# A hybrid decoder trunk on one core: gate and up with the normed input stationary, gated rows transposed on TensorE, the input by token tiles, the table's feedthrough diagonal on TensorE, later table pieces

## The chip, the core and the metric

The kernel runs on one core of a Trainium2 chip. A core has five engines that work side by side, each through its own queue in order: TensorE (PE; its weight loads are shown apart as PEld), VectorE (DVE), ScalarE (ACT), GpSimd (POOL) and SyncE (SP), which here only issues transfers. The kernel's matrix products go to PSUM tiles of 128 x 512 float32 numbers, called banks here. The metric is the device time of one execution in microseconds (us), as the median of several runs.

## The reference

A trunk of two layers over 256 tokens of width 1024, in float32. Each layer adds half of a SwiGLU, then a mixer, then half of a second SwiGLU, each on its RMS-normed input:

```
h = h + 0.5 * swiglu(rms_norm(h), w_gate, w_up, w_down)     # width 1024 -> 2816 -> 1024
h = h + mixer(rms_norm(h))                                  # layer 0: S5, layer 1: MoBA attention
h = h + 0.5 * swiglu(rms_norm(h), w_gate, w_up, w_down)

swiglu(h) = (silu(h @ w_gate) * (h @ w_up)) @ w_down
```

The S5 mixer is a diagonal state-space layer with 64 groups of 16 channels and 64 states each. It needs tables worked out from its parameters alone (powers of the transition, products of B and C, and a feedthrough diagonal d): they do not depend on the input. With 256 tokens the attention has one block of 256, and so is plain causal attention with 8 heads.

## The kernel before

There are six phases in a row: f00, s5, f01, f10, moba and f11, where an f phase is one SwiGLU. The 256 tokens are two tiles t of 128, the width has halves n of 512. `h` stays in SBUF.

**Precision by parts.** Every float32 operand of a large product is split into a high part, rounded to the format fp32r, and a low part, the rest. A product is then three: high x high, high x low and low x high. `Stream` (L38) brings the weights: SP loads blocks of 1 MB into three raw buffers (L163, L171, L177), `split` (L70) cuts each block in two halves and makes `whi` on ACT and `wlo` on DVE (L79 and L80; L85 and L86 where the norm's gain is multiplied in), in nine slots. `pump` (L93) places such a split ahead of need at fixed places in the program.

**An f phase.** The 2816 columns are 11 blocks j of 256. `gu` (L409) computes gate and up for half a block (f = 0, 1: 128 columns each): it goes through the eight k slices of 128 rows with the weights as the stationary operand and the transposed input `X` as the moving one, 256 tokens wide (L421 to L423). The output has columns on the partitions and tokens along the row. `act` (L431) multiplies it by the row of the norm's factors r (L433, DVE), takes silu of the gate half (L436, ACT), multiplies with the up half (L440, DVE), and makes the high and low part of the result (L448 ACT, L449 DVE), which are at once the stationary operands of the down product `dn` (L451), 512 wide, into four banks (L368 to L370). Since tokens lie along the row, r must be there as a row on all partitions: `rows_of_r` (L334) builds it once a phase with products of ones and a diagonal of r (L338). Because r enters only here, the products of a phase can begin before r is known. `act` waits for r's row only in the first block.

**Boundaries.** `boundary` (L346) finishes the four output banks of a phase in an order, adds them to h (L344) and transposes each piece of h for the next phase (L308), while PE works on the next bank.

**The tables.** They are built within f00. The generator `tables` (L499) is advanced by one step at every `fill(0.7)`, that is at every k step of `gu` and after every bank of `dn`; a counter of slots goes up by 0.7 each time. Its planner (L757 to L797) issues transfers at the slots LOADS, DVE work as a credit allows (DENSE per slot), and pieces for PE in `later`, which come LAG slots after the piece that they need and PACE slots apart. For each of eight blocks b: `muls` and `sums` (L507, DVE) give the tables' products; `spread` (L715) copies them with six ACT copies into padded tiles (L721 to L723) and stores two of them from POOL's queue (L725); `t3_tab` (L743) makes 16 small products on PE (L750), DVE adds the diagonal d, which `d_diag` makes on POOL (L739, L752), four ACT copies take the sum out (L754) and POOL stores it; `t1_tab` (L728), twice, transposes on PE (L732), copies on ACT (L734) and stores from POOL. The PE pieces write to the two `pR` banks, which `prep` shares. At the end the finished tables are loaded back by SP for the s5 phase.

**The start.** x comes in two loads of four transfers, one for each half n, both token tiles at once; `pre` transposes it on PE (L1173), and the first product follows when both halves and a few table inputs are in.

## Time and profile before

| | |
|---|---|
| time, median of 3 runs (lowest to highest) | 1079.3 us (1078.76 to 1079.53) |
| the profiled execution | 1078.01 us, span 1076.2 us |
| PE busy, share of the span | 1016.9 us, 94% |
| DVE / ACT / POOL busy | 720.6 / 570.7 / 168.2 us |
| mean granted clock of PE | 0.970 |
| read from memory | 182.84 MB, 183 GB/s over the span with what is written |

The profile is one execution. A line of a view gives a place in the kernel (L421 is its line 421), the engine, the operation, what it writes and reads, and durations. In a list of waits, "A <- B" says that A stood idle until B was done. In a timeline the first number is the start in us from the span's start, the second how long it took, and brackets hold the idle time before it. Products on PE are pipelined: a new one starts before the record of the last one ends, so their pace is read from start to start.

### The profile page before, as it was taken

The numbers are of one execution on the slowest core, as the hardware profiler recorded it, in microseconds if no ns is written. First come the engines' busy times: TensorE is split into PE (matmuls) and PEld (weight loads), VectorE is DVE, ScalarE is ACT, GpSimd is POOL, SyncE is SP. The second block draws the span as 40 slices with busy tenths as digits, with TensorE's granted clock in tenths as the row PEclk, the third lists the DMA queues.
The fourth block names the chain that finished last, engine by engine and source line by source line (L and its number), as shares of the span: only waits on it lengthen the run. The fifth ranks groups of instructions, "written<-read, shape, count | busy, mean of one in ns | idle before, by whom it ended". The sixth has DMA issues, their size and how long they took to land.

```text
span 1076.2 us, 17472 instructions
## 1 busy us (share of the span) xinstructions
PE 1016.9 (94%) x6853; PEld 935.6 (87%) x6853; DVE 720.6 (67%) x1176; ACT 570.7 (53%) x1024; POOL 168.2 (16%) x322
## 2 busy tenths in 40 slices
PE   6988888588999999999999999999999999999998
PEld 6977787577889989999998999999887889999997
DVE  5678576455687776766665776666578867766663
ACT  5444544555533355655553665554489656655451
POOL 6920110222156401000000100000044001000000
PEclk9989889799996999999999999999999999999999
DMA  8766555546765534565554566455344455665641
GB/s 242 204 189 206 177 194 179 181 161 211 280 217 209 203 134 155 201 202 187 196 169 145 171 224 231 158 197 195 122 157 157 156 157 180 221 226 163 205 142 40
DMA packets 137394, 197.64 MB, mean 184 GB/s; under 512 B 16272, under 2 KB 108896, under 8 KB 137056
## 3 DMA queue, kind: packets, MB, share of 16 engines
q1 hardware_dynamic: 133088, 183.16, 51.6%
q0 software_dynamic: 3616, 12.66, 3.5%
q8 instruction: 54, 0.88, 0.3%
q10 hardware_dynamic: 608, 0.71, 0.3%
q14 instruction: 28, 0.23, 0.1%
HBM read 182.84 MB, written 13.66 MB: 183 GB/s over the span
## 4 chain that ended last, share of the span: by engine, by line
PE 62%; POOL 2%; issue 1%; DVE 1%; ACT 0%; POOLq 0%; ACTq 0%
PE pM L422 11%; PE pM L421 11%; PE pM L423 11%; PE pA L370 7%; PE pA L368 7%; PE pA L369 7%; PE pM L368 1%; PE pM L370 1%; PE pM L369 1%; PE pR L308 1%; POOL qrs L281 1%; PE pA L934 0%; PE pA L935 0%; PE pA L933 0%; PE pR L1105 0%
## 5 line engine op out<-in xcount | busy, mean ns | idle before, releaser
L421 PE MATMUL pM<-xa,whi 128*128 128x256 f32 x1408 | 400.3, 284 | 0.0
L422 PE MATMUL pM<-xa,whi 128*128 128x256 f32 x1408 | 396.5, 282 | 0.0
L423 PE MATMUL pM<-xa,wlo 128*128 128x256 f32 x1408 | 396.0, 281 | 0.0
L86 DVE SCALAR_TENSOR_TENSOR wlo<-raw,gT,whi 128x512 fp32r<-128x512 f32 x328 | 228.1, 747 | 67.2 <-ACT whi L85 67.0
L421 PEld LDWEIGHTS pM<-xa,whi 128*128 128x128 f32 x1408 | 268.5, 191 | 4.6 <-issue 1.6
L422 PEld LDWEIGHTS pM<-xa,whi 128*128 128x128 f32 x1408 | 268.5, 191 | 3.2
L423 PEld LDWEIGHTS pM<-xa,wlo 128*128 128x128 f32 x1408 | 268.0, 190 | 0.0
L80 DVE TENSOR_TENSOR wlo<-raw,whi 128x1024 fp32r<-128x1024 f32 x156 | 195.2, 1262 | 83.0 <-ACT whi L79 81.9
L85 ACT ACTIVATE whi<-raw,gT 128x512 fp32r<-128x512 f32 x328 | 213.7, 711 | 18.2 <-PE pA L370 17.8
L79 ACT ACTIVATE whi<-raw 128x1024 fp32r<-128x1024 f32 x156 | 161.0, 1051 | 16.7 <-PE pA L934 9.8
L436 ACT ACTIVATE sg<-gr 128x256 f32<-128x256 f32 x88 | 36.8, 418 | 236.2 <-DVE gr L433 236.2
L368 PE MATMUL pA<-whi,ah 128*128 128x512 f32 x352 | 140.6, 399 | 0.0
L369 PE MATMUL pA<-wlo,ah 128*128 128x512 f32 x352 | 139.2, 396 | 0.0
L370 PE MATMUL pA<-whi,al 128*128 128x512 f32 x352 | 138.9, 395 | 0.0
L433 DVE TENSOR_TENSOR gr<-pM,rrow 128x512 f32<-128x512 f32 x88 | 60.5, 687 | 43.6 <-PE pM L423 43.3
L448 ACT ACTIVATE ah<-act 128x256 fp32r<-128x256 f32 x88 | 36.8, 418 | 82.1 <-DVE act L440 82.1
L370 PEld LDWEIGHTS pA<-whi,al 128*128 128x128 f32 x352 | 67.1, 191 | 14.7
L368 PEld LDWEIGHTS pA<-whi,ah 128*128 128x128 f32 x352 | 67.3, 191 | 11.1 <-issue 0.2
L369 PEld LDWEIGHTS pA<-wlo,ah 128*128 128x128 f32 x352 | 67.3, 191 | 10.8
L323 POOL TENSOR_TENSOR ms<-ss 128x1 f32<-128x1 f32 x10 | 1.9, 193 | 476.5 <-ACT sq L320 476.5
L449 DVE TENSOR_TENSOR al<-act,ah 128x256 fp32r<-128x256 f32 x88 | 37.4, 425 | 42.6 <-ACT ah L448 42.6
L440 DVE TENSOR_TENSOR act<-gr,sg 128x256 f32<-128x256 f32 x88 | 37.3, 424 | 26.5 <-ACT sg L436 26.5
(239 smaller groups left out, 1208.9 us busy)
## 6 DMA issues: line engine op xcount, KB each, us to landing
raw<-in_ffn_w_down_dram SPq DMA_DIRECT2D x44, 1024.0 KB, 5.1
raw<-in_ffn_w_gate_dram SPq DMA_DIRECT2D x80, 512.0 KB, 3.8
raw<-in_ffn_w_up_dram SPq DMA_DIRECT2D x80, 512.0 KB, 4.8
raw<-in_moba_w_qkv_dram SPq DMA_DIRECT2D x12, 1024.0 KB, 5.1
TB<-dB SPq DMA_DIRECT2D x8, 768.0 KB, 6.9
raw<-in_ffn_w_gate_dram SPq DMA_DIRECT2D x16, 256.0 KB, 4.2
raw<-in_ffn_w_up_dram SPq DMA_DIRECT2D x16, 256.0 KB, 4.5
dB<-tt POOLq DMA_DIRECT2D x16, 256.0 KB, 3.0
```

What stands on the lines that cost most here:

```text
L79: nc.scalar.activation(hi, r, AF.Copy)
L80: nc.vector.tensor_tensor(lo, r, hi.bitcast(F32), op=OP.subtract)
L85: nc.scalar.activation(hi[:, c], r[:, c], AF.Identity, scale=g)
L86: nc.vector.scalar_tensor_tensor(lo[:, c], r[:, c], g, hi[:, c].bitcast(F32), op0=OP.mult, op1=OP.subtract)
L368: mm(o, xh, wh, start=start, stop=False)
L369: mm(o, xh, wl, start=False, stop=False)
L370: mm(o, xl, wh, start=False, stop=stop)
L421: mm(o, a, xh, start=k == 0 and i == 0, stop=False, skip_group_check=True)
L422: mm(o, a, xl, start=False, stop=False, skip_group_check=True)
L423: mm(o, b, xh, start=False, stop=k == 7, skip_group_check=True)
L433: V.tensor_tensor(gr, ps.rearrange("p (i c) -> p i c", i=2), Rr["row"][:, None, :].to_broadcast([128, 2, 256]), op=OP.mult)
L449: V.tensor_tensor(al, a, ah.bitcast(F32), op=OP.subtract)
```

## The change

In an f phase, gate and up of a whole block are computed for one token tile at a time: a slice of `X` (128 rows, 128 tokens) is the stationary operand, and 512 weight columns (256 of gate, 256 of up) move past it. `gu(j, t)` takes the place of `gu(j, f)`. Tokens now lie on the partitions, so r is a number for each partition: it is the scale of silu and a factor in the DVE product that makes `act`; the diagonal and the row of r are gone. The gated rows must be turned before the down product: `tr(j, t)` transposes two 128 x 128 pieces on PE into a `pR` bank, from which ACT and DVE make the high and low parts. It stands at k = 6 of the next pass of `gu`. Of the down products, `dn(j - 2, 1)` now follows the first pass of block j and `dn(j - 1, 0)` the second.

All boundaries go by token tile, with a call for the last transpose between. x is loaded by token tiles, the first one over SP and ACT, and the products of the first tile start before the second tile is prepared, which is done in hooks of the first pass.

In the tables, the diagonal is made at the head of `spread` in two buffers and added by four small products on PE; `spread(b - 1)` comes behind the first `muls` of block b; the second half of the powers E comes last rather than after block 2; LAG is 12 rather than 9, PACE 4 rather than 3, the loads come at slots 2 to 24 rather than 3 to 36, and the generator is advanced only after slot 3. The offsets of the operands within their SBUF tiles change (XO, AO, OO).

```diff
--- before.py
+++ after.py
-XO = {'f00': 8, 's5': 124, 'g': 0, 'f01': 88, 'f10': 8, 'moba': 124, 'f11': 8}
-AO = (76, 76, 76, 76)
-OO = 76
-
-SC = (0, 0, 2, 3, 4)
-
-LOADS, C_AT, E_AT, B_AT, DENSE, LAG, PACE = (3, 6, 9, 12, 15, 18, 21, 24, 27, 30, 33, 36), 40, 26, 36, 0.46, 9, 3.0
+XO = {'f00': 124, 's5': 124, 'g': 0, 'f01': 116, 'f10': 124, 'moba': 124, 'f11': 124}
+AO = (116, 116, 116, 116)
+OO = 116
+
+LOADS, C_AT, E_AT, B_AT, DENSE, LAG, PACE = (2, 4, 6, 8, 10, 12, 14, 16, 18, 20, 22, 24), 42, 26, 36, 0.46, 12, 4.0
...
+    h2 = cp.tile([128, 2, D], F32, name="h2")
+    h = [h2[:, t, :] for t in range(2)]
+
+    def rows(t, s, c0, nc_):
+
+        return [(t * 128 + s) * D + c0, [[4 * D, 32], [1, nc_]]]
+
+    def ld_x(t, engines):
+        for s in range(4):
+            off, ap = rows(t, s, 0, D)
+            engines[s % len(engines)].dma_start(h2[s * 32:s * 32 + 32, t, :],
+                                                bass.AP(tensor=x.tensor, offset=x.offset + off, ap=ap))
+
+    ld_x(0, [nc.sync, nc.scalar])
     nc.scalar.dma_start(gn[0:32], ffn_norm.rearrange("l i (k p) -> (l i k) p", p=128))
     nc.scalar.dma_start(gn[32:48], mix_norm.rearrange("l (k p) -> (l k) p", p=128))
     warm(AF.Exp)
-    h2 = cp.tile([128, 2, D], F32, name="h2")
...
-    def diag_of_r():
-        for t in range(2):
-            Rr["diag", t] = sp.tile([128, 128], F32, name="rdiag", tag="rdiag", bufs=2)
-            nc.vector.tensor_scalar(Rr["diag", t], ident, Rr[t], None, op0=OP.mult)
-
-    def rows_of_r():
-
-        ps = psR()
-        for t in range(2):
-            mm(ps[:, t * 128:(t + 1) * 128], ones, Rr["diag", t], start=True, stop=True)
-        Rr["row"] = sp.tile([128, 256], F32, name="rrow", tag="rrow", bufs=1)
-        nc.vector.tensor_copy(Rr["row"], ps[:, 0:256])
...
-    def boundary(nxt, parts, acc, scale):
-
-        if nxt is not None and nxt[0] == "f":
-            order = [(0, 0), (1, 0), (0, 1), (1, 1)]
-        else:
-            order = [(0, 0), (0, 1), (1, 0), (1, 1)]
-        for part in parts[:-1]:
-            part(*order[0])
-            part(*order[1])
+    def boundary(nxt, parts, acc, scale, mid=None):
+
+        order = [(0, 0), (0, 1), (1, 0), (1, 1)]
+        for i in range(2):
+            for part in parts[:-1]:
+                part(*order[i])
+            if mid is not None and i == 0:
+                mid()
         for i, (t, n) in enumerate(order):
             for part in parts[-1:] if i < 2 else parts:
                 part(t, n)
...
-    def ffn(tag, nxt, entry, fill, fill0=()):
+    def ffn(tag, nxt, entry, fill):
+
         V = nc.vector
         acc = [None] * 4
-        AT = {}
-
-        def gu(j, f, hooks):
+        AT, AC = {}, {}
+
+        def gu(j, t, hooks):
             us = [where[tag, "g", j, a] for a in range(2)]
             ps = psM()
+            ts = slice(t * 128, t * 128 + 128)
             for k in range(8):
                 for fn in hooks.get(k, ()):
                     fn()
+                fill(0.7)
                 wh, wl = st.get(us[k // 4], (k % 4) // 2)
-                xh, xl = X["h"][:, k, :], X["l"][:, k, :]
-                for i in range(2):
-                    c = (k % 2) * 512 + i * 256 + f * 128
-                    o = ps[:, i * 256:(i + 1) * 256]
-                    a, b = wh[:, c:c + 128], wl[:, c:c + 128]
-                    mm(o, a, xh, start=k == 0 and i == 0, stop=False, skip_group_check=True)
-                    mm(o, a, xl, start=False, stop=False, skip_group_check=True)
-                    mm(o, b, xh, start=False, stop=k == 7, skip_group_check=True)
+                c = slice((k % 2) * 512, (k % 2) * 512 + 512)
+                mm3(ps, X["h"][:, k, ts], X["l"][:, k, ts], wh[:, c], wl[:, c], k == 0, k == 7)
                 if k % 2:
-                    if k < 7 and (j, f, k) not in ((0, 0, 1), (L, 1, 5)):
+                    if k < 7 and (j, t, k) not in ((0, 0, 1), (L, 1, 5)):
                         st.pump()
-                    if f == 1:
+                    if t == 1:
                         st.release(us[k // 4], (k % 4) // 2)
-            return ps
-
-        def act(j, f, ps):
-            gr = fp.tile([128, 2, 256], F32, name="gr", bufs=2)
-            V.tensor_tensor(gr, ps.rearrange("p (i c) -> p i c", i=2),
-                            Rr["row"][:, None, :].to_broadcast([128, 2, 256]), op=OP.mult)
             sg = fp.tile([128, 256], F32, name="sg", bufs=1)
-            nc.scalar.activation(sg, gr[:, 0, :], AF.Silu)
-            if (j, f) != (L, 1):
+            nc.scalar.activation(sg, ps[:, 0:256], AF.Silu, scale=Rr[t])
+            if (j, t) != (L, 1):
                 st.pump()
-            a = fp.tile([128, 256], F32, name="act", bufs=1)
-            V.tensor_tensor(a, gr[:, 1, :], sg, op=OP.mult)
-            if f == 0:
+            AC[t] = fp.tile([128, 256], F32, name="act", bufs=2)
+            V.scalar_tensor_tensor(AC[t], ps[:, 256:512], Rr[t], sg, op0=OP.mult, op1=OP.mult)
+
+        def tr(j, t):
+            if t == 0:
                 AT[j] = []
                 for i, n in enumerate(("ah", "al")):
                     o = AO[2 * i + j % 2]
                     a2 = fp.tile([128, 640], F32R, name=n, bufs=2)
                     AT[j].append(a2[:, o:o + 512].rearrange("p (f c) -> p f c", c=256))
-            ah, al = (x[:, f, :] for x in AT[j])
-            nc.scalar.activation(ah, a, AF.Copy)
-            V.tensor_tensor(al, a, ah.bitcast(F32), op=OP.subtract)
+            ps = psR()
+            pv = ps[:, 0:256].rearrange("p (f c) -> p f c", c=128)
+            a = AC.pop(t)
+            for f in range(2):
+                nc.tensor.transpose(pv[:, f, :], a[:, f * 128:(f + 1) * 128], ident)
+            ah, al = (x[:, :, t * 128:t * 128 + 128] for x in AT[j])
+            nc.scalar.activation(ah, pv, AF.Copy)
+            V.tensor_tensor(al, pv, ah.bitcast(F32), op=OP.subtract)
 
         def dn(j, f):
             u = where[tag, "d", j]
@@ -461,36 +442,21 @@
                 st.pump()
 
         L = NJ - 1
-        fills = {k: [lambda: fill(0.7)] for k in range(8)}
         for j in range(NJ):
+            h0 = dict(entry) if j == 0 else {6: [lambda: tr(j - 1, 1)]}
             if j == 0:
-                if fill0:
-                    p0 = gu(0, 0, fills)
-                    h1 = {k: list(v) for k, v in fills.items()}
-                    h1[1].append(diag_of_r)
-                    h1[2].append(lambda: warm(AF.Silu))
-                    h1[3].append(rows_of_r)
-                    h1[4].append(lambda: act(0, 0, p0))
-                    act(0, 1, gu(0, 1, h1))
-                    continue
-                hooks = {}
-                for k, fn in zip(SC, (lambda: None, lambda: None, diag_of_r, lambda: warm(AF.Silu), rows_of_r)):
-                    hooks.setdefault(k, []).append(fn)
-                p0 = gu(0, 0, entry)
-                hooks[rows_at := SC[4]].append(lambda: act(0, 0, p0))
-                p1 = gu(0, 1, hooks)
-                act(0, 1, p1)
-                continue
-            act(j, 0, gu(j, 0, fills))
-            dn(j - 1, 0)
-            act(j, 1, gu(j, 1, fills))
-            if j < L:
-                dn(j - 1, 1)
+                h0.setdefault(5, []).append(lambda: warm(AF.Silu))
+            gu(j, 0, h0)
+            if j > 1:
+                dn(j - 2, 1)
+            gu(j, 1, {6: [lambda: tr(j, 0)]})
+            if j:
+                dn(j - 1, 0)
 
         def part(j, f):
             return lambda t, n: bank_mm(acc, t, n, *AT[j], where[tag, "d", j], [f], False, (j, f) == (L, 1))
 
-        boundary(nxt, [part(L - 1, 1), part(L, 0), part(L, 1)], acc, 0.5)
+        boundary(nxt, [part(L - 1, 1), part(L, 0), part(L, 1)], acc, 0.5, lambda: tr(L, 1))
...
         def spread(b):
 
+            d_diag(b)
...
+        DG = {}
+
         def d_diag(b):
-            dg = tp.tile([32, 4, 32], F32, name="dg", tag="dg", bufs=1)
-            P.tensor_tensor(dg, ident[0:32, None, 0:32].to_broadcast([32, 4, 32]),
+            DG[b] = tp.tile([32, 4, 32], F32, name="dg", bufs=2)
+            P.tensor_tensor(DG[b], ident[0:32, None, 0:32].to_broadcast([32, 4, 32]),
                             dTq[0:32, 4 * b:4 * b + 4, None].to_broadcast([32, 4, 32]), op=OP.mult)
-            return dg
 
         def t3_tab(b):
             t3 = t3s[b % 2]
-            dg = d_diag(b)
             ps = psR()
             pk = ps[0:32].rearrange("p (q t c) -> p q t c", q=4, c=32)
             for qq in range(4):
                 for i in range(2):
                     mm(ps[0:32, qq * 128:(qq + 1) * 128], MPs[b % 2][:, i, qq, 3].rearrange("p g n -> p (g n)"),
-                       TTs[b % 2][:, i, qq, 0:4].rearrange("p t g n -> p (t g n)"), start=i == 0, stop=i == 1)
-            V.tensor_tensor(pk[:, :, 0, :], pk[:, :, 0, :], dg, op=OP.add)
+                       TTs[b % 2][:, i, qq, 0:4].rearrange("p t g n -> p (t g n)"), start=i == 0, stop=False,
+                       skip_group_check=True)
+                mm(pk[:, qq, 0, :], ident[0:32, 0:32], DG[b][:, qq, :], start=False, stop=True,
+                   skip_group_check=True)
             for s in range(4):
                 nc.scalar.activation(t3[32 * s:32 * s + 32, :, s:4, :], pk[:, :, 0:4 - s, :], AF.Copy)
             nc.gpsimd.dma_start(dB[b][:, 1024:1536], t3.rearrange("p q t c -> p (q t c)"))
...
-        def add_e(hf):
+        def add_e(hf, b=None):
             at = E_AT
-            for c, f in ((0.6, (e_init, hf)), (0.5, (e_step, 1)), (0.6, (e_step, 2)), (0.8, (e_step, 4)),
...
-                         (1.3, (e_step, 32, 8, 8, 0)), (0.9, (e_step, 32, 8, 8, 1)), (0.0, (e_store, hf))):
+                         (1.3, (e_step, 32, 8, 8, 0)), (0.9, (e_step, 32, 8, 8, 1)), (0.0, (e_store, hf)))):
+                if b is not None and i == 3:
+                    add_spread(b)
                 work.append((c, at, f, (), -4))
+
+        def add_spread(b):
+            work.append((0.0, B_AT, (spread, b), [(t3_tab, b), (t1_tab, b, 0), (t1_tab, b, 1)], 3 * (b - 1)))
 
         add_e(0)
         for k, w in enumerate((1.2, 1.2, 1.4)):
             work.append((w, B_AT, (b_all, k), (), -4))
         for b in range(NB):
-            for w, f in ((1.2, (muls, b, 0)), (1.2, (muls, b, 1)), (0.7, (sums, 0)), (0.7, (sums, 1))):
-                work.append((w, B_AT, f, (), 0))
-            work.append((0.0, B_AT, (spread, b), [(t3_tab, b), (t1_tab, b, 0), (t1_tab, b, 1)], 3 * (b - 1)))
-            if b == 2:
-                add_e(1)
+            for w, f in ((1.2, (muls, b, 0)), (None, b - 1), (1.2, (muls, b, 1)), (0.7, (sums, 0)), (0.7, (sums, 1))):
+                if w is not None:
+                    work.append((w, B_AT, f, (), 0))
+                elif b:
+                    add_spread(b - 1)
+        add_e(1, NB - 1)
...
     def fill(dt):
         slot[0] += dt
-        next(tab, None)
+        if slot[0] > 3.0:
+            next(tab, None)
...
+    for n in range(2):
+        squares(0, n)
+        pre(0, n)
     st.pump()
     busy(4)
     next(tab, None)
+    first = {1: [lambda: pre(1, 0)], 3: [lambda: pre(1, 1)], 5: [lambda: squares(1, 0)], 6: [lambda: squares(1, 1)]}
 
     for i, ph in enumerate(phases):
         nxt = phases[i + 1] if i + 1 < len(phases) else None
         if ph[0] == "f":
-            ffn(ph, nxt, entry_hooks(ph), fill,
-                not i)
+            ffn(ph, nxt, entry_hooks(ph) if i else first, fill)
```

37 lines of the change are left out of this document (2 added, 35 removed).

## The prediction

> **What bounds the kernel now.** The page comes first: the busy shares, the granted clock in 40 slices, and the costliest group.
>
> ```profile
> span 1076.2 us, 17472 instructions
> PE 1016.9 (94%) x6853; PEld 935.6 (87%) x6853; DVE 720.6 (67%) x1176; ACT 570.7 (53%) x1024; POOL 168.2 (16%) x322
> PEclk9989889799996999999999999999999999999999
> L421 PE MATMUL pM<-xa,whi 128*128 128x256 f32 x1408 | 400.3, 284 | 0.0
> ```
>
> TensorE (PE) is the bound, and its clock dips only in the first third. The windows by stage say where (columns: stretch, busy time of PE, PEld, DVE, ACT and POOL, granted clock, DMA share, GB/s).
>
> ```profile
> 19.00:60.00 41.00, 41.00 (x304) 39.55 (x304) 27.90 (x48) 20.47 (x28) 37.46 (x88) 0.96 0.77 219
> 60.00:262.00 202.00, 163.48 (x1087) 148.50 (x1086) 127.26 (x191) 103.46 (x180) 32.42 (x49) 0.90 0.56 185
> 400.00:586.00 186.00, 186.00 (x1339) 174.96 (x1338) 122.48 (x182) 99.12 (x164) 4.87 (x14) 1.00 0.54 182
> 586.00:773.00 187.00, 186.91 (x1344) 175.30 (x1342) 126.80 (x188) 100.17 (x167) 4.87 (x14) 1.00 0.56 187
> ```
>
> The feed-forward phases f01 and f10 run with PE full at clock 1.00, 186 us each. The first one, f00, does the same products and lasts to about 280: it also builds the S5 tables, and from 60 to 262 PE is idle 38.5 us of 202. The waits of PE between 19 and 262 (longest in total first; total, times, longest):
>
> ```profile
> PE pR L732 <- ACT t L754: 23.2, 5, 7.7
> PE pR L750 <- ACT mp L723: 6.5, 2, 4.6
> PE pR L696 <- DMA cn<-in_s_c_re_dram: 4.5, 1, 4.5
> PE pR L732 <- ACT t L734: 4.3, 2, 2.2
> ```
>
> These four sum to 38.5 us. The longest one in the timeline, engine by engine, and the clock just around it:
>
> ```profile
> 189.24 0.61 ACT L723 ACTIVATE mp<-zc 64x512 f32<-64x512 f32 x1
> 189.63 1.49 POOL L725 DMA_DIRECT2D dB<-tt  x2 [10.57 <-ACT tt L722]
> 191.13 0.41 POOL L739 TENSOR_TENSOR dg<-cst,dTq 32x128 f32<-32x128 f32 x1
> 191.58 0.29 DVE L752 TENSOR_TENSOR pR<-pR,dg 32x128 f32<-32x128 f32 x1 [4.26 <-POOL dg L739]
> 191.90 1.74 ACT L754 ACTIVATE t<-pR 32x512 f32<-32x512 f32 x4 [2.05 <-DVE pR L752]
> 193.69 1.12 PE L732 MATMUL pR<-cst,mp 128*128 128x128 f32 x4 [7.69 <-ACT t L754]
> 189.90:196.70 6.80, 3.01 (x12) 2.86 (x13) 2.24 (x3) 4.74 (x8) 2.78 (x5) 0.50 0.37 120
> ```
>
> The reader is to see a chain over four engines: the diagonal dg stands on POOL behind the stores of the next piece (L725), those wait for ACT's copies, DVE adds dg, ACT copies the sum out, and only then has PE a free pR bank. After the wait the clock stands at 0.50. Over 60 to 262 the clock costs 202 x (1 - 0.90) = 20.2 us more. So the tables cost f00 about 38.5 + 20.2 = 58.7 us.
>
> **The change part by part.** *Gate and up with 512 columns.* Start to start, the 256-wide products take (643.54 - 639.80) / 32 = 0.1169 us, the 512-wide ones (1071.59 - 1069.08) / 11 = 0.2282 us:
>
> ```profile
> 639.80 0.28 PE L421 MATMUL pM<-xa,whi 128*128 128x256 f32 x1
> 643.54 0.28 PE L423 MATMUL pM<-xa,wlo 128*128 128x256 f32 x1
> 1069.08 0.39 PE L368 MATMUL pA<-whi,ah 128*128 128x512 f32 x1
> 1071.59 0.40 PE L370 MATMUL pA<-whi,al 128*128 128x512 f32 x1
> ```
>
> 3 x 1408 = 4224 narrow products become 2112 wide ones: 2112 x (0.2338 - 0.2282) = -11.8 us, all on PE's path.
>
> *Transposes of the gated rows.* New: 11 blocks x 2 token tiles x 4 phases = 88 pairs. What a pair, a reciprocal-row product (L338, four passes) and a group of 16 table products (L750) cost in PE's stream:
>
> ```profile
> 367.73 0.39 PE L916 MATMUL pR<-cst,gs 128*128 128x128 f32 x2
> 367.87 0.36 PE L933 MATMUL pA<-xa,whi 128*128 128x256 f32 x1
> 368.07 0.28 PE L934 MATMUL pA<-xa,whi 128*128 128x256 f32 x1
> 414.97 0.61 PE L338 MATMUL pR<-rdiag,ones 128*128 128x128 f32 x4
> 415.33 0.37 PE L421 MATMUL pM<-xa,whi 128*128 128x256 f32 x1
> 415.54 0.28 PE L422 MATMUL pM<-xa,whi 128*128 128x256 f32 x1
> 177.82 1.94 PE L750 MATMUL pR<-tt,mp 128*32 128x128 f32 x16 [1.96 <-ACT mp L723]
> 179.69 0.50 PE L368 MATMUL pA<-whi,ah 128*128 128x512 f32 x1
> ```
>
> The pair holds PE 0.14 us and makes the next product 0.20 instead of 0.117: 0.223 us, so 88 x 0.223 = +19.6. The Trainium skill's page "TensorE: Matmul & The Clock Gate", Part 4 (PE-mode transpose), speaks against the change: it gives about 275 ns for a 128x128 transpose in a kernel's context. By that the 176 transposes would be 48.4 us, and the sum 28.8 us worse; the rows above do not agree, since two of them pass in 0.22 us.
>
> *Removed with the rows of r.* Four groups of L338, each 0.36 + (0.21 - 0.117) = 0.45: -1.8 us. The DVE multiply by the row (L433) goes too, but PE was full in f01 and f10, so that time is worth nothing there; what it frees is order, below.
>
> *Diagonal on PE.* 32 small products at (179.69 - 177.82) / 16 = 0.117: +3.7 us. In exchange DVE's add leaves the chain, and dg is made at the start of spread, ahead of the stores L725 on POOL. The 23.2 us wait loses its mechanism.
>
> *Later pieces.* A spread (six ACT copies, then stores) moves behind the next block's first multiply, so ACT meets sums that DVE finished earlier; pieces follow 12 slots after it rather than 9, 4 apart rather than 3 (0.7 slot is one k step, 0.68 us). This takes the ground from the 6.5 and 4.3 us waits. The twelve small loads on SP come up to twelve slots earlier, the C loads at 18 to 24 for a use at 42 instead of 27 to 36 for 40: the 4.5 us wait should go. They queue ahead of weight blocks on SP, hidden behind three raw buffers. I take the whole -38.5 and the clock's -20.2, with half as the poor end.
>
> *The wait that is new.* The pair stands at k = 6 of the next pass, 6 x 3 x 0.2282 = 4.1 us after the pass ended, and waits for act (DVE), itself behind sg and the weight split pumped between them. In f01 that chain looks so:
>
> ```profile
> 515.93 0.69 DVE L433 TENSOR_TENSOR gr<-pM,rrow 128x512 f32<-128x512 f32 x1 [0.60 <-PE pM L423]
> 516.71 0.42 ACT L436 ACTIVATE sg<-gr 128x256 f32<-128x256 f32 x1 [2.64 <-DVE gr L433]
> 517.78 1.41 DVE L86 SCALAR_TENSOR_TENSOR wlo<-raw,gT,whi 128x512 fp32r<-128x512 f32 x2 [1.16 <-ACT whi L85]
> 519.11 0.41 DVE L440 TENSOR_TENSOR act<-gr,sg 128x256 f32<-128x256 f32 x1
> 186.17 0.29 ACT L721 ACTIVATE tt<-cb 64x128 f32<-64x128 f32 x1
> 187.35 0.63 ACT L722 ACTIVATE tt<-zc 64x512 f32<-64x512 f32 x1 [0.89 <-DVE zc L507]
> 41.87 3.63 DVE L80 TENSOR_TENSOR wlo<-raw,whi 128x1024 fp32r<-128x1024 f32 x3 [0.52 <-ACT whi L79]
> ```
>
> From sg's start to act's end 519.52 - 516.71 = 2.8 us, so 1.3 us of slack for the first token tile; the second has the twelve products of a dn (2.7 us) more before its pair. In f00 a spread holds ACT from 186.17 to 189.85, 2.8 us without the 0.89 that it waits for DVE. If all of that stood ahead of sg, PE would wait 1.5 us; behind the pair stand the last two k steps, and behind its copies ah and al ACT's next splits. I let half of the eight spreads hit, 4 x 1.5 = +6 us; the ends are 0 and, with the three splits of the row at 41.87 ahead of act in some twenty early and table passes, 20 x (3.6 - 1.3) = +46.
>
> *Start and SBUF offsets.* The products begin when both halves of x and the table inputs are in:
>
> ```profile
> 11.54 1.94 PE L1173 MATMUL pA<-cst,h 128*128 128x128 f32 x8 [2.86 <-DMA h<-in_x_dram]
> 18.80 0.39 PE L421 MATMUL pM<-xa,whi 128*128 128x256 f32 x1
> ```
>
> With token tile 0 first, they could begin near 12 (up to -6.8), but then stop for the second tile and each split (1.05 on ACT, 1.22 on DVE for a third of a pass), at half clock; and two of the four loads now stand on ACT's queue ahead of gn. I take 0, ends -6.8 and +3.5. The offsets (XO, AO, OO), the order at the boundaries, where the second token tile is now wanted one pass later, and the loads of finished tables, which SP issues nearer to the end of f00: nothing in the rows prices them; 0, ends +-3, an estimate of 1 us for each.
>
> Sum against the profiled execution's 1078.0: -38.5 - 20.2 - 11.8 + 19.6 - 1.8 + 3.7 + 6 = -43.0, so **1035 us**. The median of the runs is 1.3 us above that execution, within the rounding of this sum.
>
> **The rivals.**
> - *Half of the table waits stay*, because ACT's queue, not POOL's, is what is late: half of 58.7 comes back, 1035 + 29 = 1064, less the 6 counted already: 1058. For it: ACT does splits, sg, spreads and pieces in one queue. Against: it is busy only 103 of 202 us, and the waits end at DVE and POOL rows.
> - *A pair of transposes drains PE* rather than streams: 0.39 us each, the whole record of the pair at 367.73, 88 x (0.39 - 0.22) = +15: 1050. Against: the next product starts at 367.87. The Trainium skill's figure for a transpose, named above, points the same way and would make 1064.
> - *The change does not do what it says*: every table wait stays, as the two pR banks now also serve the 22 pairs of f00. Only the PE terms remain: -11.8 + 19.6 - 1.8 + 3.7 = +9.7, so 1088.
> - *Slower: act is late for the pair in all four phases.* At each of the 44 first-tile passes three splits stand before act: 44 x (3.6 - 1.3) = 101 us over my sum without the 6, 1130. It decides from 49 / 44 = 1.1 us a pass. For it: in f00 DVE did stand behind three splits at 41.87, and the order sg, split, act is kept. Against: ACT no longer waits for DVE's gr, and in f01 the chain takes 2.8 us.
>
> **How the numbers follow.** The forecast 0.70 (its own range 1022 to 1050), half of the waits 0.12, draining pairs 0.05, no table gain 0.05, late act 0.08. The range 1020 to 1062 holds the first three, 0.87, less tails of the start and the residual waits. A change of less than 0.2% is about what cannot be told from none. Faster 0.86, same 0.01, slower 0.13.
>
> **What would show it.** Right: the f00 stage ends near 232 instead of 280; granted clock near 1.00 after 60; no wait of PE on L754's successor; 512-wide gate and up products about 0.228 apart; each pair near 0.22; f01, f10 and f11 about 1.5 us longer each. Wrong: PE waits on act at the transposes beyond a few us, or table waits with another releaser and the clock still at 0.90.

## The result and the profile after

The changed kernel takes 1066.1 us, the kernel before 1079.3 us: a ratio of 0.988 (95% interval 0.986 to 0.990). It is faster by 13 us where I had forecast 44, and 1066.1 lies outside my range of 1020 to 1062 us.

From the page of the changed kernel, the line of TensorE's busy time and the granted clock in 40 slices:

```profile
PE 1024.5 (96%) x4965; PEld 844.7 (79%) x4965; DVE 655.0 (62%) x1068; ACT 579.2 (54%) x1024; POOL 152.1 (14%) x329
...
PEclk9779999999988999999999999999999999999999
```

TensorE is still the bound. The dips of the clock have moved to the second and third slices, 27 to 80 us; the later dip, in s5, is in both kernels. The windows of the changed kernel say the same (columns as in the prediction):

```profile
13.00:62.00 49.00, 25.78 (x85) 17.85 (x85) 17.68 (x25) 16.81 (x27) 28.71 (x99) 0.74 0.46 128
62.00:250.00 188.00, 188.00 (x954) 149.08 (x953) 131.73 (x197) 116.36 (x196) 30.34 (x48) 0.99 0.69 228
```

From 62 us on, the table building that had cost the kernel before its idle time and its clock costs nothing more: PE is busy for all of 188 us (62 to 250), at clock 0.99. But from 13 to 62 us PE works only 25.8 of 49 us. There stand these waits of PE in the changed kernel (13 to 290 us; total, times, longest):

```profile
PE pR L427 <- DVE act L414: 16.0, 1, 16.0
PE pM L351 <- ACT whi L77: 5.0, 4, 1.8
PE pM L352 <- DVE wlo L78: 2.2, 4, 0.8
```

One wait holds two thirds of it. Where the stages end is read from the last four preparation transposes at each boundary (end of f00, s5, f01; timeline of PE, kernel before):

```profile
287.11 0.60 PE L308 MATMUL pR<-cst,h 128*128 128x128 f32 x4
407.37 0.60 PE L308 MATMUL pR<-cst,h 128*128 128x128 f32 x4
593.79 0.60 PE L308 MATMUL pR<-cst,h 128*128 128x128 f32 x4
```

and in the changed kernel:

```profile
271.80 0.49 PE L305 MATMUL pR<-cst,h 128*128 128x128 f32 x3
391.14 0.60 PE L305 MATMUL pR<-cst,h 128*128 128x128 f32 x4
579.08 0.60 PE L305 MATMUL pR<-cst,h 128*128 128x128 f32 x4
```

The start with f00 is shorter by 15.3 us (287.1 to 271.8), s5 by 0.9, f01 is longer by 1.5 (186.4 to 187.9). The later stages, read in the same way, are +1.4 (f10), +0.1 (moba) and +1.6 (f11). So the three f phases behind f00 came out as forecast, and the stretch up to the end of f00 is the place of the error: -47.5 forecast (-58.7 for waits and clock, +1.5 for the PE terms of a phase, +3.7 diagonal, +6 for the new wait), -15.3 measured.

### The profile page after: what moved, and what is told of

Its sections match the earlier page's. It is cut to its first block, busy times and chain, and to the rows that moved or that the text cites. A ratio compares the mean times of both kernels' runs of the same rounds, so it can differ in the third digit from the quotient of the medians.

```text
span 1064.7 us, 13634 instructions
## 1 busy us (share of the span) xinstructions
PE 1024.5 (96%) x4965; PEld 844.7 (79%) x4965; DVE 655.0 (62%) x1068; ACT 579.2 (54%) x1024; POOL 152.1 (14%) x329
## 4 chain that ended last, share of the span: by engine, by line
PE 87%; POOL 5%; DVE 3%; issue 3%; ACT 1%; DMA 1%; ACTq 0%; SPq 0%; POOLq 0%; DVEq 0%
PE pM L351 16%; PE pM L352 16%; PE pM L353 16%; PE pA L351 9%; PE pA L353 9%; PE pA L352 9%; PE pR L427 2%; PE pR L717 2%; PE pM L820 1%; PE pR L305 1%; POOL qrs L278 1%; PE pA L908 1%; PE pA L909 1%; PE pA L910 1%; DMA h<-in_x_dram 1%
## 5 line engine op out<-in xcount | busy, mean ns | idle before, releaser
L351 PE MATMUL pM<-whi,xa 128*128 128x512 f32 x832 | 342.1, 411 | 5.0 <-ACT whi L77 5.0
L352 PE MATMUL pM<-wlo,xa 128*128 128x512 f32 x832 | 328.7, 395 | 2.2 <-DVE wlo L78 2.2
L353 PE MATMUL pM<-whi,xa 128*128 128x512 f32 x832 | 327.8, 394 | 0.0
L83 ACT ACTIVATE whi<-raw,gT 128x512 fp32r<-128x512 f32 x328 | 217.2, 714 | 71.6 <-PE pA L353 62.5
L351 PEld LDWEIGHTS pM<-whi,xa 128*128 128x128 f32 x832 | 158.2, 190 | 35.4 <-ACT whi L77 6.7
L353 PEld LDWEIGHTS pM<-whi,xa 128*128 128x128 f32 x832 | 157.9, 190 | 34.7
L352 PEld LDWEIGHTS pM<-wlo,xa 128*128 128x128 f32 x832 | 158.4, 190 | 32.4 <-DVE wlo L78 4.1
L429 ACT ACTIVATE ah<-pR 128x256 fp32r<-128x256 f32 x88 | 33.7, 383 | 128.9 <-PE pR L427 128.7
L410 ACT ACTIVATE sg<-pM,rr 128x256 f32<-128x256 f32 x88 | 41.7, 474 | 97.1 <-PE pM L353 76.9
L430 DVE TENSOR_TENSOR al<-pR,ah 128x256 fp32r<-128x256 f32 x88 | 37.0, 421 | 72.7 <-ACT ah L429 72.7
L414 DVE SCALAR_TENSOR_TENSOR act<-pM,rr,sg 128x256 f32<-128x256 f32 x88 | 42.3, 480 | 46.9 <-ACT sg L410 46.9
L427 PE MATMUL pR<-cst,act 128*128 128x128 f32 x176 | 33.9, 274 | 16.0 <-DVE act L414 16.0
```

The costliest lines, as they stand in the source:

```text
L83: nc.scalar.activation(hi[:, c], r[:, c], AF.Identity, scale=g)
L351: mm(o, xh, wh, start=start, stop=False)
L352: mm(o, xh, wl, start=False, stop=False)
L353: mm(o, xl, wh, start=False, stop=stop)
L410: nc.scalar.activation(sg, ps[:, 0:256], AF.Silu, scale=Rr[t])
L414: V.scalar_tensor_tensor(AC[t], ps[:, 256:512], Rr[t], sg, op0=OP.mult, op1=OP.mult)
```

## The experiments

None of the fifteen kernels leaves out a part of the reference. The time of the kernel before beside them was 1078.0 to 1079.2 us.

### r of token tile 1 ahead of the tables

The 16 us wait, followed back in the timeline of the changed kernel:

```profile
27.80 0.45 POOL L513 TENSOR_TENSOR e<-prm 128x32 f32<-128x32 f32 x2 [12.53 <-DVE dTq L504]
...
56.29 0.20 POOL L320 TENSOR_TENSOR ms<-ss 128x1 f32<-128x1 f32 x1
...
58.33 0.19 POOL L282 TENSOR_TENSOR rr<-rr,rs_e 128x1 f32<-128x1 f32 x1
58.56 0.47 ACT L410 ACTIVATE sg<-pM,rr 128x256 f32<-128x256 f32 x1 [17.94 <-POOL rr L282]
...
61.68 0.69 PE L427 MATMUL pR<-cst,act 128*128 128x128 f32 x2 [16.01 <-DVE act L414]
```

ACT's sg of the second token tile waits 17.9 us for r of that tile, POOL computes it at 56.3 to 58.5, and until then POOL works through the parameters of the tables, begun at 27.8 us. In the changed kernel the squares of tile 1 are issued at k = 5 and 6 of the first pass, and the parameters' chain, all of it at once, at k = 5, just ahead of the last square. The edit lets the chain come later:

```diff
-        if slot[0] > 3.0:
+        if slot[0] > 4.5:
             next(tab, None)
```

> Edit: the changed kernel with the gate of fill at slot 4.5 instead of 3.0, so that POOL computes r of token tile 1 (L320, L321, rsq) ahead of the table parameters' chain and not behind it; nothing else moves but the three first steps of the tables, by two k steps. POOL theory: the 16.0 us wait of PE for act before the second pair of transposes is the wait for r of tile 1, and the 2.7 us of half clock behind it are its echo; both go, 18.7 us, so 1066.1 - 18.7 = 1047 us, and the chain of waits at 62 us has no L414. Rival, late splits: in the first passes DVE and ACT are behind with splits and table work anyway, act comes little earlier, and the time stays above 1060. Rival, displaced chain: the parameters are ready later and the first E pieces or the dB stores wait in turn, 1052 to 1058.

Measured: 1047.4 us (ratio 0.971, 0.970 to 0.973), 18.7 us less than the changed kernel. The timeline of this run:

```profile
30.08 0.62 POOL L320 TENSOR_TENSOR ms<-ss 128x1 f32<-128x1 f32 x1 [14.44 <-ACT sq L317]
...
32.67 0.44 POOL L513 TENSOR_TENSOR e<-prm 128x32 f32<-128x32 f32 x2
```

POOL makes r at 30 us and begins the parameters behind it. What is left of waits for act (L414) is 1.9 us in two places. The chain of tables begins 5 us later, and no table wait comes up for it (the waits of PE from 13 to 290 us are those for act and for the first pass's splits). The POOL theory holds in full; both rivals are out.

### The two halves of the change, each alone at the old start

The change has a feed-forward part and a table part; both with the kernel before's start (x by halves, both tiles prepared and r computed ahead of the first pass). First the whole change at the old start:

```diff
-    ld_x(0, [nc.sync, nc.scalar])
+    ld_x(0, [nc.sync])                  # x by halves of 512 columns, as before
...
-    for n in range(2):
-        squares(0, n)
-        pre(0, n)
+    for t in range(2):
+        square(t, 0)
+    pv = [pre(t, 0) for t in range(2)]
...
```

> Edit: the changed kernel with the start of the kernel before: x by halves of 512 columns for both token tiles, both tiles prepared ahead of the first pass, r of both in one POOL chain ahead of the table parameters. Gate and up, transposes and tables stay changed. By the trace, TensorE lost 20.3 us up to 45 us in the changed kernel and 10.4 in the kernel before, so the start by token tiles costs 9.9 us beside the wait for r. Theory: 1066.1 - 18.7 - 9.9 = 1037.5 us. Rival, the start by token tiles is not at fault (the lateness is that of the weights): 1047 us, as with r alone.

Then the tables alone, in the kernel before:

```diff
-LOADS, ... = (3, 6, ..., 36), 40, 26, 36, 0.46, 9, 3.0
+LOADS, ... = (2, 4, ..., 24), 42, 26, 36, 0.46, 12, 4.0
...
+            d_diag(b)
             tv, mv = ...
...
-            V.tensor_tensor(pk[:, :, 0, :], pk[:, :, 0, :], dg, op=OP.add)
+                mm(pk[:, qq, 0, :], ident[0:32, 0:32], DG[b][:, qq, :], start=False, stop=True, ...)
...
+                    add_spread(b - 1)
```

> Edit: the kernel before with the table part of the change alone: the diagonal on TensorE, dg ahead of the stores, spreads one multiply later, the new LOADS, C_AT, LAG and PACE, the gate of fill; to fit in SBUF dtb and dg share two buffers. Gate and up stay as they were (256 columns, r's rows by TensorE). Theory of the double count: between 60 and 290 us the kernel before lost 50.4 us against the usual cadence, 38.5 of it waits and about 12 the half clock while TensorE was busy (my 20.2 also counted the half clock under the waits); so 1079.3 - 50 + 3.7 for the diagonal = 1033 us. Rival, the sum as predicted: 1079.3 - 58.7 + 3.7 = 1024 us. Rival, the tables gain only because the changed feed-forward relieves ACT and DVE: 1050 us or more.

And the feed-forward part alone (the same lines of tables undone in the run with the old start):

> Edit: the kernel before with the feed-forward part alone: gate and up with the normed input stationary, gated rows transposed on TensorE, the boundary order and the SBUF offsets of the changed kernel; start and tables as before. By the terms of the sum: -11.8 for the wide products, +19.6 for the pairs, -1.8 for the rows of r, so 1079.3 + 6 = 1085 us if the table waits stay what they were. Rival: without the multiply by r's row on DVE and with act on one engine less, table waits shrink by themselves: 1060 to 1075 us. Rival: the pair's copies make ACT and DVE later for the tables: 1090 us or more.

| at the old start | tables before | tables changed |
|---|---|---|
| feed-forward before | 1078.5 | 1042.0 (0.966, 0.965 to 0.967) |
| feed-forward changed | 1061.4 (0.984, 0.982 to 0.985) | 1045.1 (0.969, 0.967 to 0.970) |

All three sums missed. The whole change at the old start was expected at 1037.5 us and takes 1045.1. The tables alone bring 36.5 us, not 46 or 55. The feed-forward alone, which I had priced as a loss of 6 us, brings 17. Together they bring less than the tables alone, but that comparison is not clean: both kernels of the lower row lose some 5 us in f01 and f10 for a reason of their own (f01 lasts 191.5 us in each of them, 187.9 in the changed kernel), which the next section takes up. Without that loss the whole change at the old start takes 1039.1 us, 3 us less than the tables alone. The waits of PE in the run with the feed-forward alone (60 to 262 us):

```profile
PE pR L699 <- ACT t L721: 11.6, 4, 4.2
PE pR L699 <- DVE al L431: 4.7, 2, 2.5
```

Of 38.5 us of table waits 16.3 are left with the old tables: the rival "without the multiply by r's row the waits shrink by themselves" holds. The two halves of the change take away the same waits, so their gains, 36.5 and 17 us, do not add up, with 1039.1 us either. Which part of the feed-forward shrinks the waits was not run apart. And in the run with the tables alone a wait has come up that neither kernel has, PE for ACT's copies of C's transposes (60 to 290 us):

```profile
PE pR L696 <- ACT cb L699: 10.5, 2, 7.5
```

In that run TensorE loses 12 us against its usual cadence between 60 and 80 us, so by that estimate the tables alone would stand near 1030 us without it; the run that tried to get there, further down, did not.

The longer f01 is the next experiment.

### Where the operands lie in SBUF

In the run with the old start nothing of f01 had been edited, but 512-wide products came 0.233 us apart: (452.00 - 449.90) / 9 in its timeline,

```profile
449.90 0.39 PE L354 MATMUL pM<-whi,xa 128*128 128x512 f32 x1
...
452.00 0.40 PE L354 MATMUL pM<-whi,xa 128*128 128x512 f32 x1
```

against (452.83 - 450.09) / 12 = 0.228 us in the changed kernel:

```profile
450.09 0.39 PE L351 MATMUL pM<-whi,xa 128*128 128x512 f32 x1
...
452.83 0.39 PE L351 MATMUL pM<-whi,xa 128*128 128x512 f32 x1
```

What differs is that the start before holds its squares and r in small tiles of its own, ss4, ms2 and rr2, in the pool that lies ahead of the feed-forward's. Two runs test it. One makes the old start with the changed kernel's small tiles:

```diff
-    ss4 = sp.tile([128, 2, 2], F32, ...); def square(t, n): ...
-    for t in range(2):
-        square(t, 0)
+    for t in range(2):
+        squares(t, 0)
...
-    v2, r2 = ...; rsq(r2, v2, 2)
```

> Edit: as the run with the old start, but the squares and r of both tiles are made by the changed kernel's own function, so that the pool of small tiles, which lies in SBUF ahead of the pool of ah and al, keeps its size. In the run with the old start the stages f01, f10 and f11 were 5.1, 2.8 and 3.0 us longer than before instead of 1.5, 1.4 and 1.6, and the down products came every 232 to 238 ns instead of 227 to 229, though nothing there had been edited. Placement theory: about 40 bytes more in the small pool moved ah and al against the place that the offsets AO were set for; with the old size the three stages come back to +1.5 and the run to 1045.1 - 6.7 - some 2 in f00 = 1036 us, and the start by halves is worth 1047.4 - 1036 = 10 us or a little more. Rival: the cadence is set by something else (which weight buffers the stages meet after another start), the stages stay at +5.1 and +2.8, 1045 us.

The other takes the run of 1047.4 us and gives it the old offsets:

```diff
-XO = {'f00': 124, 's5': 124, 'g': 0, 'f01': 116, 'f10': 124, 'moba': 124, 'f11': 124}
-AO = (116, 116, 116, 116)
-OO = 116
+XO = {'f00': 8, 's5': 124, 'g': 0, 'f01': 88, 'f10': 8, 'moba': 124, 'f11': 8}
+AO = (76, 76, 76, 76)
+OO = 76
```

> Edit: the changed kernel with r of tile 1 ahead of the tables (the run of 1047.4 us), and in it the offsets XO, AO and OO of the kernel before, nothing else. My prediction took them at 0 with ends of 3 us. Placement theory: offsets and pools belong together, so the old offsets in the new pools give the 232 to 238 ns cadence in some of the stages; from 1 to 5 us for each of f00, f01, f10 and f11, 1051 to 1067 us. Rival, offsets without weight: 1047 us, and all cadences 227 to 229.

Measured: 1039.1 us (0.963, 0.961 to 0.965) for the first, 6 us less than with the old small tiles and 3 more than expected; 1059.6 us (0.982, 0.980 to 0.983) for the second, 12.2 us more than with the new offsets, where nothing but the offsets was edited. The ends of s5 and f01 with the old start and the changed kernel's small tiles,

```profile
363.01 0.49 PE L306 MATMUL pR<-cst,h 128*128 128x128 f32 x3
...
550.90 0.49 PE L306 MATMUL pR<-cst,h 128*128 128x128 f32 x3
```

with the old start and its own small tiles,

```profile
362.85 0.49 PE L306 MATMUL pR<-cst,h 128*128 128x128 f32 x3
...
554.35 0.60 PE L306 MATMUL pR<-cst,h 128*128 128x128 f32 x4
```

and with the old offsets:

```profile
373.99 0.49 PE L305 MATMUL pR<-cst,h 128*128 128x128 f32 x3
...
564.79 0.49 PE L305 MATMUL pR<-cst,h 128*128 128x128 f32 x3
```

f01 takes 187.9, 191.5 and 190.8 us. So the small tiles, by my count of their sizes a shift of some tens of bytes, cost 3.6 us in a stage of 188, and the line of offsets in the diff, priced by me at 0 with ends of 3 us, keeps 12 us. It isn't a gain over the kernel before, whose cadence was 0.228 too: the offsets go with the pools, and whoever changes the pools has to set them anew. What in the address decides was not tried.

The same two runs price the start: 1047.4 - 1039.1 = 8.3 us between the start by token tiles and the start by halves, r's wait left out. (The first slots of the tables differ by two k steps between them as well.)

### What the start by token tiles costs

The first pass in the run of 1047.4 us: first product, one of the stops for splits, first pair of transposes.

```profile
15.70 0.50 PE L351 MATMUL pM<-whi,xa 128*128 128x512 f32 x1 [1.77 <-ACT whi L77]
26.37 0.50 PE L351 MATMUL pM<-whi,xa 128*128 128x512 f32 x1 [1.33 <-ACT whi L77]
36.96 0.33 PE L427 MATMUL pR<-cst,act 128*128 128x128 f32 x1 [0.39 <-DVE act L414]
```

and in the placed run with the start by halves:

```profile
14.49 0.77 PE L352 MATMUL pM<-whi,xa 128*128 128x512 f32 x1
...
26.80 0.38 PE L428 MATMUL pR<-cst,act 128*128 128x128 f32 x2
```

The first products differ by 1.2 us, the first pairs by 10.2. Two runs, each with one edit to the run of 1047.4 us, ask whether the loads or the order of preparation do it:

```diff
-    ld_x(0, [nc.sync, nc.scalar])
     nc.scalar.dma_start(gn[0:32], ...)
     nc.scalar.dma_start(gn[32:48], ...)
+    ld_x(0, [nc.sync, nc.scalar])
```

> Edit: the changed kernel with r of tile 1 ahead of the tables (1047.4 us), and in it the two gn loads stand ahead of the two x loads on ACT's queue, as in the kernel before. In the run of 1047.4 us the first transpose of gn comes at 10.0 us and the first product at 15.7; in the placed run with the old start they come at 5.9 and 14.5, and the first pair of transposes at 36.96 and 26.80. Theory, order of preparation: the loads carry no more than the 1.2 us between the first products, since TensorE then stops for ACT's and DVE's splits; 1046 to 1048 us. Rival, loads: gn four us earlier brings everything forward, 1042 to 1044 us.

```diff
+    for n in range(2):
+        squares(1, n)
+        pre(1, n)
     st.pump()
     busy(4)
     next(tab, None)
-    first = {1: [lambda: pre(1, 0)], 3: [lambda: pre(1, 1)], 5: ..., 6: ...}
+    first = {}
```

> Edit: the changed kernel with r of tile 1 ahead of the tables (1047.4 us), and in it the squares and the preparation of token tile 1 stand ahead of the first pass, behind those of tile 0; x still comes by token tiles on two queues. Theory, order of preparation: in the first pass ACT and DVE have only the splits left, so TensorE goes through without stops and at full clock, as in the start by halves; 4 to 8 us of the 8 come back: 1039 to 1043 us. Rival, loads: tile 1 comes last on SP, the first product moves to 18 us or more, and what the pass gains the later beginning takes: 1046 to 1049 us.

Measured: 1046.5 us with gn first (0.970, 0.969 to 0.971), 1043.4 with both tiles ahead (0.967, 0.966 to 0.969). With gn first, the first product and the first pair:

```profile
13.52 0.79 PE L351 MATMUL pM<-whi,xa 128*128 128x512 f32 x1 [1.77 <-ACT whi L77]
...
36.60 0.38 PE L427 MATMUL pR<-cst,act 128*128 128x128 f32 x2
```

The products begin 2.2 us earlier and the pass ends 0.4 earlier: the stops for the splits take it back. With both tiles ahead:

```profile
19.38 0.67 PE L351 MATMUL pM<-whi,xa 128*128 128x512 f32 x1 [5.21 <-ACT whi L77]
...
33.88 0.44 PE L427 MATMUL pR<-cst,act 128*128 128x128 f32 x2 [0.39 <-DVE act L414]
```

the products begin 3.7 us later and the pass ends 3.1 earlier. So of the 8.3 us, 4 come back when tile 1 is prepared ahead of the first pass, in which it had held up ACT's and DVE's splits; the queue place of gn is worth 1 us at most. The other 4 are a difference, not an experiment of their own: I put them to x by token tiles, whose second tile comes last, and that is not shown.

### What took the table waits away

My argument was the diagonal: dg made ahead of the stores on POOL, no add on DVE. The edit makes the diagonal as in the kernel before, in the run of 1047.4 us:

```diff
-            d_diag(b)                                    # in spread
...
+            dg = d_diag(b)                               # in t3_tab
-                mm(pk[:, qq, 0, :], ident[0:32, 0:32], DG[b][:, qq, :], start=False, stop=True, ...)
+            V.tensor_tensor(pk[:, :, 0, :], pk[:, :, 0, :], dg, op=OP.add)
```

> Edit: the changed kernel with r of tile 1 ahead of the tables (1047.4 us), and in it the diagonal of D as in the kernel before: dg made by POOL in t3_tab, added by DVE, no products for it on TensorE. The later pieces, LAG and PACE stay. Theory of my prediction: dg behind the stores on POOL and DVE's add make the copy late for the pR bank, so a part of the 23.2 us comes back, against 3.7 us of products saved: 1050 to 1066 us, with waits of PE for L720's successor. Rival: it was the spacing (12 slots after the spread, 4 apart) that took the waits away, and the diagonal on TensorE only costs: 1047.4 - 3.7 = 1043.7 us.

Measured: 1040.3 us (0.964, 0.962 to 0.965), 7.1 us faster than with the diagonal on TensorE. The rival holds, and by more than it asked. The pieces of one block in TensorE's timeline, from their first product to the first one behind them, with the diagonal on TensorE:

```profile
109.04 0.62 PE L717 MATMUL pR<-tt,mp 128*32 128x128 f32 x4
109.60 0.24 PE L720 MATMUL pR<-dg,cst 32*32 32x32 f32 x2
...
111.95 0.50 PE L351 MATMUL pM<-whi,xa 128*128 128x512 f32 x1
```

and with it on DVE, and the group of the successor in that run (60 to 290 us; busy, mean ns of one, idle before it):

```profile
110.82 1.93 PE L716 MATMUL pR<-tt,mp 128*32 128x128 f32 x16
112.69 0.50 PE L351 MATMUL pM<-whi,xa 128*128 128x512 f32 x1
...
L698 PE MATMUL pR<-cst,mp 128*128 128x128 f32 x64 | 9.7, 274 | 0.3 <-ACT t L720 0.3
```

The waits do not come back: 0.3 us before the successor. And the diagonal lengthens a block's piece from 1.87 to 2.91 us, so eight blocks by 8.3 us. Each product of these small ones leaves two records (the 16 records of a block are eight products in the program), so the 32 products of the diagonal are 64 records, at 0.13 us each. The best parts together, the placed run with the start by halves and this diagonal:

> Edit: the run with the old start and the placed pools (1039.1 us), and in it the diagonal on DVE as in the kernel before. The diagonal on TensorE cost 1047.4 - 1040.3 = 7.1 us in the other start. Theory, the parts add up: 1039.1 - 7.1 = 1032 us, without waits of PE in the table pieces. Rival: with the products 8 us earlier the DVE add stands behind splits and the pieces wait, 1036 us or more.

Measured: 1030.6 us (0.956, 0.955 to 0.958), against 1032 expected. The parts add up, and this version beats both kernels. From there two runs undo the planner's changes, one each:

```diff
-... 0.46, 12, 4.0
+... 0.46, 9, 3.0
```

> Edit: the best parts (wide gate and up, old start, placed pools, diagonal on DVE), and in it LAG 9 and PACE 3.0 as in the kernel before; spreads stay one multiply later. Spacing theory: since the diagonal on DVE waits for nothing, it is the 12 slots after the spread and the 4 between pieces that took the table waits away; with 9 and 3 PE waits again for ACT's copies of the pieces, 10 to 30 us with the clock: 1042 to 1062 us. Rival, the place of the spreads does it: 1032 us within 2.

```diff
-            for w, f in ((1.2, (muls, b, 0)), (None, b - 1), (1.2, (muls, b, 1)), ...
-                elif b:
-                    add_spread(b - 1)
-        add_e(1, NB - 1)
+            for w, f in ((1.2, (muls, b, 0)), (1.2, (muls, b, 1)), ...
+            work.append((0.0, B_AT, (spread, b), ...))
+            if b == 2:
+                add_e(1)
```

> Edit: the best parts, and in it the spreads and the second E half at the places they had in the kernel before (spread right behind its own sums, E after block 2); LAG 12 and PACE 4 stay. Theory, place of the spreads: ACT stands at the spread for DVE's sums with the split or sg behind it, and PE waits again, for splits or copies: 1040 to 1055 us. Rival, the spacing alone does it: 1032 us within 2.

Measured: 1044.0 us with the old spacing (0.968, 0.965 to 0.972), 1039.9 with the old places of the spreads (0.963, 0.960 to 0.965); their runs scatter by 8 us (1040.6 to 1048.3 and 1034.8 to 1042.9), those of the others by 4 at most. The largest waits in the one, in its profiled execution,

```profile
PE pR L699 <- ACT t L721: 4.8, 3, 2.5
PE pR L428 <- ACT t L721: 3.1, 2, 2.1
```

and in the other (both 60 to 270 us):

```profile
PE pR L428 <- ACT t L721: 4.3, 2, 3.8
```

Undoing either costs 9 to 13 us, so it is spacing and place together, not one of them, that empty the waits; with that scatter, which of the two weighs more stays open. With both in place the diagonal plays no part in the wide form. Whether it would help there with the old spacing was not run. Here the pR banks are what the pair of gated rows (L428) and the table pieces compete for.

### The narrow form with the new planner

> Edit: as the run with the tables alone, with C_AT 40 as in the kernel before instead of 42 (LOADS stay early). In that run TensorE lost 12.4 us between 60 and 80 us at the transposes of C: two waits, 10.5 us, for ACT's copies L699, and half clock behind them, since the third transpose group met the copies behind sg of the pass. Theory, a matter of where in the pass the groups fall: three slots earlier the copies stand elsewhere, the 12 us go, and the tables alone give 1042.0 - 12 = 1030 us, better than both kernels. Rival: with r's rows and gr on DVE, C's copies wait in ACT's queue at any slot; the wait moves and stays, 1038 to 1046 us.

```diff
-LOADS, C_AT, ... = (2, 4, ..., 24), 42, ...
+LOADS, C_AT, ... = (2, 4, ..., 24), 40, ...
```

Measured: 1043.0 us (0.967, 0.965 to 0.968), no better than with 42. The waits at C's transposes fall from 10.5 to 3.4 us and one for ACT's copy of a piece comes up (60 to 252 us):

```profile
PE pR L733 <- ACT t L757: 5.8, 1, 5.8
```

That is the rival, "the wait moves and stays".

> Edit: the kernel before (narrow gate and up, r's rows by TensorE, old start) with the new places of spreads and pieces, the diagonal left on DVE, and C's transposes 4 slots apart from slot 36 on instead of 1.4 apart from 40 or 42. The narrow form saves 4.5 us in f01, f10 and f11 and 1.5 in f00 against the wide one with its pairs. Theory, the waits at C's transposes (10.5 us and half clock behind them in the run with the tables alone) come from four groups inside three k steps: 1042.0 - 12 - 7 = 1023 us, the best of all. Rival: in the narrow form ACT's queue is held by sg behind DVE's gr, so that pieces wait wherever they stand: 1032 to 1042 us.

```diff
-LOADS, C_AT, E_AT, ... = (3, 6, ..., 36), 40, 26, 36, 0.46, 9, 3.0
+LOADS, C_AT, E_AT, ... = (2, 4, ..., 24), 36, 26, 36, 0.46, 12, 4.0
...
-        later = [(C_AT + 1.4 * k, c_tr) + divmod(k, 2) for k in range(4)]
+        later = [(C_AT + PACE * k, c_tr) + divmod(k, 2) for k in range(4)]
```

Measured: 1049.7 us (0.973, 0.972 to 0.975), a clear miss of my 1023. Its largest wait (13 to 270 us):

```profile
PE pR L732 <- ACT t L754: 12.6, 3, 7.2
```

That is the very wait of the kernel before. In the narrow form, with DVE adding the diagonal behind gr, the places of the pieces alone do not remove it; in the wide form they do. The two narrow runs with the diagonal on TensorE have none of this wait (C_AT 42) and 5.8 us of it (C_AT 40), and are about 7 us faster than this one. So in the narrow form my argument for the diagonal may hold; the runs also differ in where C's transposes stand, and the diagonal on TensorE with spaced transposes was not run.

The last run gave x's first half to two queues in the best version:

```diff
-    ld_x(0, [nc.sync])
+    ld_x(0, [nc.sync, nc.scalar])
```

> Edit: the best parts (1030.6 us), and in it the first half of x comes over SP's and ACT's queues in turn instead of SP's alone. Theory: the first transposes wait 0.5 us and the second ones 2.5 us for x, so two loads that leave SP's queue bring the second half and the raw weights some 1 us forward; 1028 to 1030 us. Rival: the loads share the same DMA engines and gn comes later behind or beside them; 1030 to 1033 us.

Measured: 1031.4 us (0.956, 0.955 to 0.958), no difference from 1030.6.

## Why the prediction was right or wrong

The sum is 31 us short of the measured 1066.1 us. The step that failed most is the start, which I took at 0: moving token tile 1 into the first pass put r of that tile behind the table parameters on POOL, and the run that puts r ahead of them is 18.7 us faster. The rest is spread over the terms below.

**Right: the PE terms of a phase.** Wide products -2.95, pairs +4.9, rows of r -0.45 make +1.5 us a phase; f01, f10 and f11 are +1.5, +1.4 and +1.6. A pair in f01 of the changed kernel:

```profile
453.52 0.38 PE L427 MATMUL pR<-cst,act 128*128 128x128 f32 x2
453.65 0.48 PE L351 MATMUL pM<-whi,xa 128*128 128x512 f32 x1
453.97 0.40 PE L352 MATMUL pM<-wlo,xa 128*128 128x512 f32 x1
```

It holds PE 0.13 us and makes the next product 0.32 instead of 0.228: 0.22 us, as taken from the neighbouring rows. The rival that pairs drain PE is out, and with it the 275 ns for each transpose of the Trainium skill ("TensorE: Matmul & The Clock Gate", Part 4), which does not hold in this stream.

**Right in outcome, wrong in cause: the table waits.** All 38.5 us are gone, but not by "*Diagonal on PE* ... the 23.2 us wait loses its mechanism": with the diagonal back on DVE the waits stay away. In the changed kernel it was no help and costs 7 to 8.5 us (1047.4 - 1040.3, 1039.1 - 1030.6), not 3.7. The term counted 32 products at the time of one record, 0.117 us; they are 64 records. The waits went by spacing and place of the pieces, which I had set against the smaller waits alone, and in part by the changed feed-forward, which leaves 16.3 of the 38.5 us with the old tables and to which my sum gave no credit for tables at all. That all of them went is in part luck: the step with the largest credit was not the one that did it.

**Wrong in size: the half clock, -20.2.** I multiplied the clock's deficit with the whole stretch, idle time included. The half-clock stretches of the kernel before between 60 and 262 us, of seven the fifth, and their sum (windows):

```profile
189.94:196.77 6.83, 3.08 (x13) 2.89 (x14) 2.31 (x3) 4.81 (x8) 2.74 (x5) 0.50 0.39 124
...
sum 40.97, PE 29.39 PEld 26.57 DVE 25.37 ACT 25.63 POOL 10.84; mean PE 4.20 PEld 3.80 DVE 3.62 ACT 3.66 POOL 1.55
```

PE works 29.4 of those 41.0 us, so by estimate the half rate cost half of that, 14.7 us; the other 5.8 were idle time that I had already counted among the waits. The Trainium skill ("TensorE: Matmul & The Clock Gate", Terms) has the same rule, a penalty of throttled time x (1 - K/N), here 40.97 x 0.5 = 20.5 us by estimate. The trace does not agree where PE idles inside the throttled time.

**Wrong: "I take 0, ends -6.8 and +3.5" for the start.** One mechanism was missing from that step and one was priced too low. The squares of tile 1 move behind the parameters' chain on POOL, and I had not asked what POOL's queue holds at that place: 18.7 us. The Trainium skill ("TensorE: Matmul & The Clock Gate", the table at its head) has strict first-in first-out queues for ACT, DVE and POOL; the rows at 27.80 and 56.29 agree, since r starts only when the chain is through. The one priced too low I did name, "then stop for the second tile and each split, at half clock", and set against the earlier begin; with its price and the rest of the start it is 8.3 us, beyond my end.

**Offsets, 0 with ends of 3.** In the changed kernel they belong to its pools and cost nothing against before, so the 0 stands; but the bound was wrong, since 12 us hang on them.

**The new wait, +6.** For the mechanism that I described (spreads and splits ahead of act) 1.9 us, in the run of 1047.4 us. The 16 us at the same instruction have another cause.

The balance of f00 and the start, in us:

| term | forecast | measured | miss |
|---|---|---|---|
| r of tile 1 behind the tables on POOL | none | +18.7 | +18.7 |
| start | 0 | +8.3 | +8.3 |
| half clock | -20.2 | -14.7 (estimate) | +5.5 |
| diagonal on TensorE | +3.7 | +7.8 (mean of two) | +4.1 |
| wait of the pair for act | +6 | +1.9 | -4.1 |
| sum of the misses | | | +32.5 |

The stage missed by 47.5 - 15.3 = 32.2 us. That the two agree so closely is partly chance: the half clock is an estimate, the diagonal was measured at two starts, and the terms are differences of runs of which each scatters by up to 4 us.

## What to carry to other kernels

When a small calculation is moved, write down for each in-order queue what already stands at its new place: seven instructions of 0.2 to 0.6 us that slip behind 28 us of table arithmetic cost 18.7 us, though POOL is busy for 14% of the span. Price a product by the records that it leaves in the trace. Count a lowered clock only over the time in which the engine works, and expect two edits that remove the same wait to gain less than their sum. Where offsets into SBUF are part of a kernel, any edit that changes a pool's size must be timed with the cadence of the untouched stages beside it.

## What the hardware showed that I had not expected

The place of operands in SBUF decides between 0.228 and 0.233 us for the same 512-wide product, about 3 us in a stage of 188, with no wait and no lower clock in the rows.

The half clock came after less idle time than I had thought needed. The windows of the kernel before around its wait of 2.14 us at 127.4 us:

```profile
125.09:128.50 3.41, 1.27 (x12) 1.14 (x11) 2.93 (x5) 2.99 (x5) 0.54 (x1) 1.00 0.30 120
...
128.50:131.91 3.41, 3.41 (x10) 2.73 (x10) 2.44 (x4) 0.93 (x2) 0.00 (x0) 0.50 0.80 252
```

A stretch of 3.41 us in which PE was busy for 1.27 was followed by one at half clock.
